# Expert weights in tiles of 2 MiB, with 16 KiB in a row, in a decoder block on one core

## The chip, the core and the metric

The kernel runs on one core of a Trainium2 chip. The metric is the device time of one execution in microseconds; the time of the kernel before is the median of three runs. A profile of one execution gives the trace from which the rows below are read.

## The reference

One block of a decoder for 256 tokens of 1024 features, in float32. What matters here is its last third, a mixture of experts:

```python
def hier_moe(xn, w_rg, b_rg, w_re, b_re, w_e_gate, w_e_up, w_e_down):
    ...                                   # group: top 1 of 8; expert: top 2 of 8 in it
    def expert_block(a):
        xb, e = a
        hdn = jax.nn.silu(xb @ w_e_gate[e]) * (xb @ w_e_up[e])
        return hdn @ w_e_down[e]
    ...

h = h + token_mixer(rmsnorm(h), ...)           # gated unit over tokens beside causal attention
h = h + mem_cross_attention(rmsnorm(h), ...)
h = h + hier_moe(rmsnorm(h), ...)              # 64 experts: gate and up 1024 x 512, down 512 x 1024
return rmsnorm(h, norm_final)
```

The weights of the first two thirds are 48 MiB, those of the 64 experts 384 MiB, 6 MiB each.

## The kernel before, in words

**Dense stage.** The products of the mixers and of the cross-attention read their weights in 48 pieces of 1 MiB (8 KiB in each of 128 partitions), in the order of the list ORDER (line 68). Each piece is split on ScalarE and VectorE into a rounded part and its rest (`split`, line 233), and three passes on PE make the product (`feature_out`, line 282, `token_out`, line 300).

**Expert stage.** 16 groups of four experts (GE = 4, line 39). Each expert has 32 slots for tokens, so four experts fill the array's columns side by side, 32 each. For a group PE gathers its tokens (line 815), makes gate and up (`pg` and `pu`, line 965: eight chunks of rows, for each chunk four experts), turns the hidden rows (line 852), makes the down product (`py`, line 986) and adds the weighted rows to the tokens' sums (line 862). In most groups the innermost loop of both products goes over the four experts. In the last group the down product goes by three blocks of columns (BLOCKS, line 48), and there the loop goes over the experts, and for each over two chunks of rows (line 1031). Its sums then run through the final norm (lines 905 to 935). Products that nothing reads (`keep_warm`, line 175) stand before and between the last ones (lines 1028, 1035, 1038).

**Loads.** All weights form one list, `pieces` (lines 98 to 115): for a group four experts' gate and up, each half the rows of an expert (four rows of 2 KiB that follow each other in HBM, 8 KiB), then the down weights (two rows of 4 KiB in two places). The last group's down pieces are cut by blocks of columns, with rows of 2 and 1 KiB. `pump` (line 119) issues the next pieces on SyncE's queue (SP) as long as slots are free; `take` and `done` count them. Weights and activations share one ring of slots, NBIG = 20 of 8 KiB in a partition (line 80), and from the expert stage on there are NBIG2 = 3 more (line 722). Caps (`cap`, CAPS) hold the number of slots with weights down in the dense stage. SP works in order: a transfer that waits for its slot, or for an earlier transfer to land, holds back all that is queued behind it. At the start, `xT` and the first two pieces come in parts by chunks of rows (FIRST, line 51), then piece 2, then the residual `h` (line 164), then more pieces. `h` is needed for the first rms (`squares`, line 268, called from line 354).

Of the kernel before, what the change touches and what calls it, by code (L numbers as in the profile page):

```python
# [29 lines left out]
P = 128  # L30
# [23 lines left out]

# The dense weights in pieces of 1 MiB: as they are packed, and in the order of their use.
PACKED = [("v", 4), ("u", 4), ("wa", 4), ("g", 8), ("k", 4), ("q", 4), ("va", 4), ("wb", 4), ("wo", 4),
          ("xk", 2), ("xq", 2), ("xv", 2), ("xo", 2)]


def _dense_index(name, i):  # L60
    base = 0
    for n, c in PACKED:
        if n == name:
            return base + i
        base += c
# [9 lines left out]
def block_kernel(ctx, tc, x, xt, mem, memt, wp, par, wrp, brt, wsp, bsp, rel, oneh, gfin, weg, weu, wed, out):  # L75
# [12 lines left out]
    def slot(name, shape=(P, 2048), dtype=F32, kind="a"):  # L88
# [9 lines left out]
    pieces = [(wp[_dense_index(name, i)], (P, 2048)) for name, i in ORDER]  # L98
    def up_pieces(w, g, h):
        """Half h of the rows of four experts: a piece per expert, or per chunk of rows at the start."""  # L100
        ws = w[g * GE:(g + 1) * GE].rearrange("e (p k) n -> p e k n", p=P)[:, :, 4 * h:4 * h + 4, :]
        if g == 0 and h == 0 and w is weg:
            return [(ws[:, :, k], (P, GE, EH)) for k in range(4)]
        return [(ws[:, e], (P, 4, EH)) for e in range(GE)]

    def down_pieces(g):
        """Halves of the rows; at the end also by blocks of columns."""
        ws = wed[g * GE:(g + 1) * GE].rearrange("e (j p) n -> p e j n", p=P)
        return [(ws[:, e, 2 * h:2 * h + 2, lo:hi], (P, 2, hi - lo))
                for lo, hi in (BLOCKS if g + 1 == NGRP else [(0, D)]) for h in range(2) for e in range(GE)]  # L110

    for g in range(NGRP):
        for h in range(2):
            pieces += up_pieces(weg, g, h) + up_pieces(weu, g, h)
        pieces += down_pieces(g)
    loaded = {}
    nxt, used, cap = [0], [0], [6]

    def pump():
        while nxt[0] < len(pieces):  # L120
# [6 lines left out]
            src, shape = pieces[nxt[0]]  # L127
            t = slot("w", shape, kind=kind)
            nc.sync.dma_start(t, src)  # L129
            loaded[nxt[0]] = (t, kind)  # L130
            nxt[0] += 1

    taken = []

    def take():
        i = used[0]
        used[0] += 1
        t, kind = loaded.pop(i)
        taken.append(kind)
        return t  # L140
# [12 lines left out]
    xT = slot("xT", (P, KC, T))  # L153
    for k0, k1 in FIRST:
        i = k0 // 4
        if k0 % 4 == 0:
            loaded[i] = (slot("w", kind="w"), "w")
        cs = slice(k0 % 4 * 512, (k0 % 4 + k1 - k0) * 512)
        nc.sync.dma_start(xT[:, k0:k1], xt[:, k0:k1])
        nc.sync.dma_start(loaded[i][0][:, cs], pieces[i][0][:, cs])  # L160
    nxt[0] = 2
    cap[0] = 3
    pump()
    nc.sync.dma_start(h, x.rearrange("(t p) d -> p t d", p=P))
    cap[0] = 6
# [9 lines left out]
    def keep_warm(ps, n):  # L175
        """Products that nothing reads: the array's clock falls to half when it idles."""
# [37 lines left out]
    with ExitStack() as ph:  # L214
# [11 lines left out]
        def after_split():  # L226
            """What the block traces on the two engines queues behind the newest split."""
# [5 lines left out]
        def split(src, shape):  # L233
            """A weight block as a float32r part and the float32r rest."""
# [8 lines left out]
        def parts(hi, lo, src, scale=None):  # L243
            """src (PSUM or SBUF) * scale, split into float32r parts."""
# [8 lines left out]
        def to_features(xs, gam, hi, lo, pairs):  # L253
            """Token-major [P, 2, D] -> feature-major parts [P, KC, T], times gam, for pairs of chunks."""
# [13 lines left out]
        def squares(src, ss):  # L268
            """Sum of squares of src [P, 1024] to ss [P, 1]."""
# [3 lines left out]
        def row_of(r, name):  # L273
            """r [P tokens, 2] as a row of 256 on every partition."""
# [7 lines left out]
        def feature_out(c, xh, xl, evac, between=()):  # L282
            """x @ W, feature-major: two 128-feature tiles of a piece of W."""
# [16 lines left out]
        def token_out(c, kpieces, xh, xl, evac, before=None, step=SPLIT_K // 2):  # L300
            """x @ W, token-major: 512 columns, K over pieces of 4 chunks."""
# [24 lines left out]
        xh, xl = slot("xh", (P, KC, T), F32R), slot("xl", (P, KC, T), F32R)  # L326
# [9 lines left out]
        wb = slot("wb", (P, 2, D))  # L336
        wspt = wb[:, 0].rearrange("p (g t) -> p g t", g=8)
        bspt = wb[:, 1].rearrange("p (g t) -> p g t", g=8)
        nc.sync.dma_start(wb[:, 0], wsp)
        nc.sync.dma_start(wb[:, 1], bass.AP(tensor=bsp.tensor, offset=bsp.offset, ap=[[0, P], [1, D]]))  # L340
# [4 lines left out]
        vg = slot("vg", (P, 2, D))  # L345
# [15 lines left out]
        drop()  # L361
# [15 lines left out]
        uT = slot("uT", (P, KC, T))  # L377

# [20 lines left out]
        bias = slot("bias", (P, HEADS, 256))  # L399
# [5 lines left out]
        gates = [slot("g0", (P, KC, T)), slot("g1", (P, KC, T))]  # L405
# [8 lines left out]
        uh, ul = slot("uh", (P, KC, T), F32R), slot("ul", (P, KC, T), F32R)  # L414
# [31 lines left out]
        drop(3)  # L446

# [1 line left out]
        va = slot("va", (P, 2, D))  # L449
# [6 lines left out]
        kT = slot("kT", (P, HEADS, T))  # L456
        qT = slot("qT", (P, HEADS, T))
# [8 lines left out]
        ah, al = slot("ah", (P, HEADS, T), F32R), slot("al", (P, HEADS, T), F32R)  # L466
# [44 lines left out]
        for i in range(12):  # L511
# [12 lines left out]
            if i == 7:  # L524
                drop(2)
                cap[0] = CAPS[0]
            if 3 <= i <= 10:
                mix_values(i - 3)
        drop(6)

# [1 line left out]
        cap[0] = CAPS[1]  # L532
        pump()
        mm_, mT = slot("mem", (P, 2, D)), slot("mT", (P, KC, T))
        nc.sync.dma_start(mT, memt)
        nc.sync.dma_start(mm_, mem.rearrange("(t p) d -> p t d", p=P))
        mh, ml = slot("mh", (P, KC, T), F32R), slot("ml", (P, KC, T), F32R)
# [10 lines left out]
        drop(4)  # L548
# [4 lines left out]
        cap[0] = CAPS[2]  # L553
        for c in range(2):
            token_out(c, 2, mh, ml, add_h)
        nh, nl = slot("nh", (P, KC, T), F32R), slot("nl", (P, KC, T), F32R)
# [7 lines left out]
        drop(4)  # L564
        cap[0] = CAPS[3]
        pump()

# [1 line left out]
        kv = slot("kv", (P, 2, D))  # L569
        kxT = kv[:, 0].rearrange("p (h t) -> p h t", h=XHEADS)  # L570
        vx = kv[:, 1].rearrange("p (m n) -> p m n", m=2)
# [4 lines left out]
        yh, yl = slot("yh", (P, KC, T), F32R), slot("yl", (P, KC, T), F32R)  # L576
        cap[0] = CAPS[4]
# [14 lines left out]
        pr4 = slot("pr", (P, XHEADS, 2, T))  # L592
# [55 lines left out]
        drop(2)  # L648
        cap[0] = NBIG
        pump()  # L650
        token_out(0, 2, nh, nl, vx_evac, beside_vx)
        drop(2)
# [51 lines left out]
        drop(2)  # L704
# [28 lines left out]
    # constants of the routing  # L733
# [10 lines left out]
    G.iota(io64, pattern=[[-1, NE]], base=NE, channel_multiplier=0, allow_small_or_imprecise_dtypes=True)  # L744
# [450 lines left out]
```

## Time and profile before

| | |
|---|---|
| time, median of 3 runs | 1257.06 us (1256.94 to 1258.0) |
| span of the profiled execution | 1254.8 us |
| PE busy | 954.4 us, 76% |
| PE weight loads busy | 525.8 us, 42% |
| VectorE, ScalarE busy | 258.1 us, 224.9 us |
| GpSimd busy | 21.5 us, 52 instructions |
| DMA packets, bytes | 90014, 463.31 MB |
| read from HBM over the span | 370 GB/s |

The table's busy times are means over the whole span, and the kernel has two stages of different kind, so the slices, the windows and the chain of work say more. In the slices each digit is the busy share of a fortieth of the span in tenths. Times of PE's instructions have modelled ends and overlap. [...]

### The profile page before, as it was taken

Reading aid. Unit: us, or ns where it says so; the run is one execution under the profiler, and the core shown is the slowest. Engines: PE = TensorE matmul, PEld = TensorE weight load, DVE = VectorE, ACT = ScalarE, POOL = GpSimd, SP = SyncE. Lnnn points to the kernel's source line nnn. Section 1 sums busy time; section 2 is a strip of 40 time slices with the busy share of each in tenths; the row PEclk is TensorE's granted clock in tenths of the full one; section 3 lists DMA queues with packets and bytes.
Section 4 is the critical chain, followed back from the end, with each engine's and each line's share of the span. In section 5 each row is a group of like instructions: output and inputs, shape, how many; then the busy total and the mean of one; then the engine's idle time right before and its main releaser. Section 6 shows DMA issues by size and latency. Waiting matters only on the chain.

```text
span 1254.8 us, 14523 instructions
## 1 busy us (share of the span) xinstructions
PE 954.4 (76%) x6167; PEld 525.8 (42%) x6167; DVE 258.1 (21%) x480; ACT 224.9 (18%) x372; POOL 21.5 (2%) x52
## 2 busy tenths in 40 slices
PE   8999999999897667667575758484848576756676
PEld 7998999898443122121222222222222222221223
DVE  5656676776200000000000000000000000000002
ACT  6455554664100000000000000000000000000002
POOL 0010000000000000000000000000000000000000
PEclk9999999999998888787888878888979787878889
DMA  9696258848999999999999999999999999999995
GB/s 352 252 359 232 102 198 316 291 142 294 389 416 418 416 418 415 420 413 420 413 421 413 421 413 422 413 421 413 421 413 420 414 420 415 418 416 417 417 404 179
DMA packets 90014, 463.31 MB, mean 369 GB/s; under 512 B 7857, under 2 KB 14809, under 8 KB 51674
## 3 DMA queue, kind: packets, MB, share of 16 engines
q1 hardware_dynamic: 89658, 461.96, 91.6%
q8 instruction: 49, 0.80, 0.3%
q10 hardware_dynamic: 288, 0.39, 0.1%
q14 instruction: 19, 0.16, 0.0%
HBM read 461.26 MB, written 2.63 MB: 370 GB/s over the span
## 4 chain that ended last, share of the span: by engine, by line
DMA 59%; PE 37%; SPq 2%; DVE 1%; ACT 1%; issue 0%; DVEq 0%; ACTq 0%
DMA w<-in_weg 30%; DMA w<-in_weu 16%; DMA w<-in_wed 12%; PE acc L294 5%; PE acc L296 5%; PE acc L295 5%; PE pg L965 3%; PE py L986 3%; PE pu L965 3%; PE acc L315 2%; PE acc L316 2%; PE acc L314 2%; SPq L129 2%; PE xp L815 1%; PE a L862 1%; PE a L1009 1%
## 5 line engine op out<-in xcount | busy, mean ns | idle before, releaser
L965 PE MATMUL pg<-w,xg 128*32 128x512 f32 x1024 | 213.7, 701 | 212.5 <-DMA w<-in_weg 212.4
L965 PE MATMUL pu<-w,xg 128*32 128x512 f32 x1024 | 186.0, 647 | 51.0 <-DMA w<-in_weu 50.8
L965 PEld LDWEIGHTS pg<-w,xg 128*32 128x32 f32 x1024 | 42.3, 124 | 343.8 <-DMA w<-in_weg 258.7
L849 DVE SCALAR_TENSOR_TENSOR ws<-pu,cw,ws 128x512 f32<-128x512 f32 x16 | 12.0, 751 | 744.0 <-ACT ws L848 414.3
L986 PE MATMUL py<-w,ws 128*32 128x512 f32 (+1 forms) x1056 | 161.9, 693 | 0.3 <-ACT ws L853 0.3
L239 DVE TENSOR_TENSOR lo<-w,hi 128x1024 fp32r<-128x1024 f32 (+1 forms) x102 | 120.6, 1183 | 68.6 <-ACT hi L237 68.2
L237 ACT ACTIVATE hi<-w 128x1024 fp32r<-128x1024 f32 (+1 forms) x102 | 102.7, 1008 | 115.3 <-PE acc L295 78.7
L965 PEld LDWEIGHTS pu<-w,xg 128*32 128x32 f32 x1024 | 45.0, 117 | 165.5 <-DMA w<-in_weu 91.3
L294 PE MATMUL acc<-xh,hi 128*128 128x256 f32 x320 | 91.7, 287 | 0.0
L848 ACT ACTIVATE ws<-pg,cw 128x512 f32<-128x512 f32 x16 | 11.0, 687 | 445.3 <-PE pu L965 277.9
L295 PE MATMUL acc<-xl,hi 128*128 128x256 f32 x320 | 90.5, 283 | 0.0
L296 PE MATMUL acc<-xh,lo 128*128 128x256 f32 x320 | 90.4, 283 | 0.0
L986 PEld LDWEIGHTS py<-w,ws 128*32 128x32 f32 x1056 | 45.7, 122 | 101.2 <-issue 94.9
L860 ACT ACTIVATE ws<-py 128x512 f32<-128x512 f32 (+1 forms) x33 | 19.3, 584 | 306.1 <-PE py L986 306.1
L815 PE MATMUL xp<-gt,h 128*128 128x128 f32 x512 | 62.3, 280 | 0.6 <-DVE gt L799 0.6
L815 PEld LDWEIGHTS xp<-gt,h 128*128 128x128 f32 x512 | 60.3, 196 | 3.3 <-issue 2.5
L294 PEld LDWEIGHTS acc<-xh,hi 128*128 128x128 f32 x320 | 61.2, 191 | 0.7 <-issue 0.6
L295 PEld LDWEIGHTS acc<-xl,hi 128*128 128x128 f32 x320 | 61.3, 192 | 0.1
L296 PEld LDWEIGHTS acc<-xh,lo 128*128 128x128 f32 x320 | 61.2, 191 | 0.0
L862 PE MATMUL a<-ws,cw 128*128 128x512 f32 (+1 forms) x128 | 58.6, 599 | 1.2 <-ACT ws L860 1.2
L862 PEld LDWEIGHTS a<-ws,cw 128*128 128x128 f32 x128 | 22.9, 189 | 37.2 <-issue 22.0
L816 DVE TENSOR_TENSOR xg<-xp,prm 128x512 f32<-128x512 f32 (+2 forms) x35 | 22.6, 646 | 61.0 <-PE xp L815 61.0
(288 smaller groups left out, 905.0 us busy)
## 6 DMA issues: line engine op xcount, KB each, us to landing
w<-in_weg SPq DMA_DIRECT2D x128, 1024.0 KB, 19.8
w<-in_weu SPq DMA_DIRECT2D x128, 1024.0 KB, 19.9
w<-in_wed SPq DMA_DIRECT2D x120, 1024.0 KB, 20.0
w<-in_wp SPq DMA_DIRECT2D x46, 1024.0 KB, 9.9
w<-in_wed SPq DMA_DIRECT2D x8, 512.0 KB, 15.4
w<-in_wed SPq DMA_DIRECT2D x16, 256.0 KB, 6.3
w<-in_wp SPq DMA_DIRECT2D x3, 512.0 KB, 8.1
skew<-brow SPq DMA_DIRECT2D x1, 1536.0 KB
```

The costliest lines, as they stand in the source:

```text
L129: nc.sync.dma_start(t, src)
L237: newest[0] = S.activation(hi, src, AF.Copy)
L239: newest[1] = V.tensor_sub(lo, src, hi.bitcast(F32))
L294: PE.matmul(ps[:, m], wh[:, k - k0], xh[:, k], start=(k == 0), stop=False)
L295: PE.matmul(ps[:, m], wh[:, k - k0], xl[:, k], start=False, stop=False)
L296: PE.matmul(ps[:, m], wl[:, k - k0], xh[:, k], start=False, stop=(k == KC - 1))
L314: PE.matmul(ps[t], xh[:, k, ts], wh[:, j], start=first, stop=False)
L315: PE.matmul(ps[t], xh[:, k, ts], wl[:, j], start=False, stop=False)
L815: PE.matmul(xp[:, k], h[:, t, (k0 + k) * P:(k0 + k + 1) * P], gt[:, t], start=(t == 0), stop=(t == 1))
L862: mm = PE.matmul(dst[t], cw[:, t * P:(t + 1) * P], ws[:, lo:hi], start=first, stop=last)
L965: PE.matmul(po_[es_], xg[:, 4 * hh + k, es_], wk[:, e] if by_chunk else wg[e][:, k], start=(hh == 0 and k == 0), stop=(hh == 1 and k == 3))
L986: return PE.matmul(py[es_], hT[:, j, es_], wd, start=(j == 0), stop=(j == 3))
```

## The change

The host packs the weights anew, and the kernel loads them in tiles of 2 MiB, with 16 KiB in a row for each partition.

- *Experts.* A tile holds, for four experts at once, a quarter of the rows of gate, of up or of down: 12 tiles in a group, in HBM one behind the other (`wq`). The last group's down weights are packed by the blocks of columns (`wz`): two tiles for block 0, one for block 1, and one for block 2, which is loaded in four transfers of 512 KiB with 4 KiB in a row.
- *Dense.* Two of the 1 MiB pieces form a tile, in the order of their use. The first comes in chunks as before, the second in two halves, and `h` is issued behind them.
- *Buffers.* The ring has 11 slots of 16 KiB, and one more in the expert stage. Activations of 8 KiB are put in one slot by pairs. `ws`, the rows beside the hidden product, gets a buffer of its own. CAPS count tiles. The memory that is set aside for GpSimd's own DMA descriptors goes from its default to 128 bytes in a partition.
- *Order on PE.* Gate is done before up for all rows, tile by tile; the down products of the last group go over chunks, and for each chunk over the experts. The fillers between the last products fall away; six before the last block stay.
- *Branch for tokens beyond 32 of an expert* (taken only where there are such tokens): it finds its expert's rows by a row number, for which one more iota is made.

The diff, cut to its core:

```diff
-NBIG = 20
-NBIG2 = 3
+NBIG = 11
+NBIG2 = 1
+SCRATCH = 128
-CAPS = (9, 12, 14, 15, 14)
+CAPS = (5, 6, 7, 7, 8)
-WARM_END = (6, 3)
+WARM_END = 6
...
+    def pair(name, dtype=F32, shape=(KC, T)):
+        t = slot(name, (P, 2) + shape, dtype)
+        return t[:, 0], t[:, 1]
...
+    tiles = [((P, 2, 2048), [(slice(0, 2), wp[i])], 2) for i in range(len(ORDER) // 2)]
+    tiles += [((P, GE, 1024), [(slice(0, GE), wq[g, i])], 1) for g in range(NGRP) for i in range(12 if g + 1 < NGRP else 8)]
+    tiles += [((P, 2, 2048), [(slice(0, 2), wz[i].rearrange("p (j n) -> p j n", j=2))], 1) for i in range(2)]
+    tiles += [((P, 4, 1024), [(slice(0, 4), wz[2].rearrange("p (j n) -> p j n", j=4))], 1)]
+    tiles += [((P, 4, 1024), [(j, wz[3][:, j * 1024:(j + 1) * 1024]) for j in range(4)], 1)]
...
-    nxt[0] = 2
-    cap[0] = 3
+    nxt[0] = 1
+    cap[0] = 2
+    tiles[1][1][:] = [(i, wp[1][:, i]) for i in range(2)]
     pump()
     nc.sync.dma_start(h, x.rearrange("(t p) d -> p t d", p=P))
-    cap[0] = 6
+    cap[0] = CAPS[0]
     pump()
...
-    xh, xl = slot("xh", (P, KC, T), F32R), slot("xl", (P, KC, T), F32R)
+    xh, xl = pair("xhl", F32R)
...
+    ws = mt("ws", [P, 1536])
...
-        for hh in range(2):
-            for po_ in (pg, pu):
-                by_chunk = g == 0 and hh == 0 and po_ is pg
-                wg = [] if by_chunk else [take() for _ in range(GE)]
...
+        for po_ in (pg, pu):
+            for c in range(4):
+                w = take().rearrange("p e (k n) -> p e k n", k=2)
+                for k in range(2):
                     for e in range(GE):
                         es_ = slice(SLOTS * e, SLOTS * (e + 1))
+                        PE.matmul(po_[es_], xg[:, 2 * c + k, es_], w[:, e, k], start=(c + k == 0), stop=(c == 3 and k == 1))
+                done()
+                if g == 0 and po_ is pg and c < 3:
+                    gather_chunks(xg, gt, 2 * c + 2, 2)
...
-            for hh in range(2):
-                wd = [take() for _ in range(GE)]
-                for j in range(2):
+            for j in range(4):
+                wd = take()
...
                     if at_end:
-                        idle = ps_t.tile([P, P], F32, tag="t", name="idle")
-                        keep_warm(idle, WARM_END[0])
-                    for hh in range(2):
-                        wd = [take() for _ in range(GE)]
-                        for e, j in [(e, j) for e in range(GE) for j in range(2)]:
-                            mm = down(2 * hh + j, py, e, wd[e][:, j])
-                            if at_end and j and e < hh * 3:
-                                with tc.issue_after(mm.ins):
-                                    keep_warm(idle, 1)
-                        if at_end and not hh:
-                            with tc.issue_after(mm.ins):
-                                keep_warm(idle, WARM_END[1])
+                        keep_warm(ps_t.tile([P, P], F32, tag="t", name="idle"), WARM_END)
+                    js = 4096 // (GE * (hi - lo))
+                    for j0 in range(0, 4, js):
+                        wd = take().rearrange("p j (e n) -> p j e n", e=GE)
+                        for j in range(js):
+                            for e in range(GE):
+                                mm = down(j0 + j, py, e, wd[:, j, e])
                         done()
...
+    up = lambda w: w.reshape(NGRP, GE, P, 4, 2 * EH).transpose(0, 3, 2, 1, 4)
+    wdn = w_e_down[0].reshape(NGRP, GE, 4, P, D).transpose(0, 2, 3, 1, 4)
+    wq = np.concatenate([up(w_e_gate[0]), up(w_e_up[0]), wdn], axis=1)
```

## Rows read from the trace of the kernel before

**Rows 1.** The page's slices of PE and DMA, 40 of 31.4 us.

```profile
PE   8999999999897667667575758484848576756676
DMA  9696258848999999999999999999999999999995
```

**Rows 2.** The page's chain that ended last, by engine and by line.

```profile
DMA 59%; PE 37%; SPq 2%; DVE 1%; ACT 1%; issue 0%; DVEq 0%; ACTq 0%
DMA w<-in_weg 30%; DMA w<-in_weu 16%; DMA w<-in_wed 12%; PE acc L294 5%; PE acc L296 5%; PE acc L295 5%; PE pg L965 3%; PE py L986 3%; PE pu L965 3%; PE acc L315 2%; PE acc L316 2%; PE acc L314 2%; SPq L129 2%; PE xp L815 1%; PE a L862 1%; PE a L1009 1%
```

**Rows 3.** Windows: length, busy us (instructions), granted clock, DMA share, GB/s.

```profile
320.00:324.00 4.00, 4.00 (x33) 2.07 (x32) 1.65 (x8) 0.00 (x0) 0.76 (x2) 1.00 0.84 276
...
880.00:940.00 60.00, 37.10 (x246) 13.40 (x242) 2.56 (x5) 2.87 (x5) 0.76 (x2) 0.87 1.02 417
1206.00:1214.00 8.00, 6.62 (x30) 1.49 (x30) 0.00 (x0) 0.00 (x0) 0.00 (x0) 0.57 1.01 412
...
1238.00:1248.00 10.00, 8.22 (x46) 4.12 (x42) 1.12 (x7) 2.02 (x8) 0.00 (x0) 1.00 0.03 8
```

**Rows 4.** The DMA view from 938 to 966 us, up weights alone.

```profile
DMA packets 1617, 11.80 MB, mean 421 GB/s; under 512 B 178, under 2 KB 178, under 8 KB 178
```

**Rows 5.** The DMA view from 972 to 988 us, down weights alone.

```profile
DMA packets 1663, 6.53 MB, mean 408 GB/s; under 512 B 100, under 2 KB 100, under 8 KB 1633
```

**Rows 6.** SP's timeline: start, length; down transfers of two groups.

```profile
896.86 21.85 SPq L129 DMA_DIRECT2D w<-in_wed  x8
...
957.29 21.65 SPq L129 DMA_DIRECT2D w<-in_wed  x8
```

**Rows 7.** SP's own waits: us in total, times, longest.

```profile
SPq L129 <- DMA w<-in_weg: 239.2, 114, 3.4
```

**Rows 8.** The page's DMA issues: KB each, median us to landing.

```profile
w<-in_weg SPq DMA_DIRECT2D x128, 1024.0 KB, 19.8
```

**Rows 9.** SP's timeline where the expert stage begins.

```profile
299.77 22.26 SPq L129 DMA_DIRECT2D w<-in_wed  x8
323.75 7.88 SPq L129 DMA_DIRECT2D w<-in_weg  x4
```

**Rows 10.** The timeline at the start, around the first rms.

```profile
7.59 0.71 SPq L164 DMA_DIRECT2D h<-in_x  x1
...
19.14 1.04 ACT L271 ACTIVATE junk<-h 128x1024 bf16<-128x1024 f32 x1
...
22.99 2.36 DVE L239 TENSOR_TENSOR lo<-w,hi 128x1024 fp32r<-128x1024 f32 x2
...
25.14 0.48 PE L314 MATMUL acc<-hi,xh 128*128 128x512 f32 x1
```

**Rows 11.** The view of the tile `h`, 0 to 60 us.

```profile
DMA to landing us min/median/max: 11.3/11.3/11.3
```

**Rows 12.** The chain that ended last, in order of time, its end.

```profile
1197.05 20.16 DMA w<-in_weu
...
1223.48 6.32 PE py L986 x31
...
1230.48 1.98 PE a L862 x4
...
1236.27 1.34 PE idle L178 x12
...
1239.05 0.86 PE idle L178 x6
...
1240.89 0.42 PE idle L178 x2
...
1244.11 0.99 PE py L986 x4
```

**Rows 13.** The same chain in the first group.

```profile
349.58 6.87 PE py L986 x64
```

**Rows 14.** The page's DMA queues: packets, MB, share of 16 engines.

```profile
q8 instruction: 49, 0.80, 0.3%
```

More of the change, by code (lines that the diff above doesn't have):

```diff
@@ L74, in block_kernel @@
 @with_exitstack
-def block_kernel(ctx, tc, x, xt, mem, memt, wp, par, wrp, brt, wsp, bsp, rel, oneh, gfin, weg, weu, wed, out):
+def block_kernel(ctx, tc, x, xt, mem, memt, wp, par, wrp, brt, wsp, bsp, rel, oneh, gfin, wq, wz, out):
     nc = tc.nc
@@ L93, in slot @@
         return pool.tile(list(shape), dtype, tag="big", name=f"{name}_{made[0]}")
+    def pair(name, dtype=F32, shape=(KC, T)):
+        t = slot(name, (P, 2) + shape, dtype)
+        return t[:, 0], t[:, 1]
     def drop(n=1, kind="a"):
         live[kind] -= n
[L98 to L115, printed above, removed]
+    tiles = [((P, 2, 2048), [(slice(0, 2), wp[i])], 2) for i in range(len(ORDER) // 2)]
[3 more added lines that the diff above has]
+    tiles += [((P, 4, 1024), [(j, wz[3][:, j * 1024:(j + 1) * 1024]) for j in range(4)], 1)]
     loaded = {}
-    nxt, used, cap = [0], [0], [6]
+    nxt, used, cap = [0], [0], [3]
     def pump():
-        while nxt[0] < len(pieces):
+        while nxt[0] < len(tiles):
             if extra and live["x"] < NBIG2:
@@ L126, in pump @@
                 break
-            src, shape = pieces[nxt[0]]
+            shape, transfers, pieces = tiles[nxt[0]]
             t = slot("w", shape, kind=kind)
-            nc.sync.dma_start(t, src)
-            loaded[nxt[0]] = (t, kind)
+            for at, src in transfers:
+                nc.sync.dma_start(t[:, at], src)
+            loaded[nxt[0]] = (t, kind, pieces)
             nxt[0] += 1
     taken = []
+    halves = [0]
     def take():
[L136 to L140, printed above, removed]
+        t, kind, pieces = loaded[used[0]]
+        at = halves[0]
+        halves[0] = (at + 1) % pieces
+        if not halves[0]:
+            del loaded[used[0]]
+            used[0] += 1
+            taken.append(kind)
+        return t[:, at] if pieces > 1 else t
     def done():
@@ L744, in block_kernel @@
     G.iota(io64, pattern=[[-1, NE]], base=NE, channel_multiplier=0, allow_small_or_imprecise_dtypes=True)
+    row64 = mt("row64", [P, NE])
+    G.iota(row64, pattern=[[12 * P * GE, NGRP], [1, GE]], base=0, channel_multiplier=0, allow_small_or_imprecise_dtypes=True)
+    rows = wq.rearrange("g c p e n -> (g c p e) n")
     tri = mt("tri", [P, 2, P], BF16)
@@ L1074, in block_kernel, with expert_tile @@
             V.tensor_sub(jobs, jobs, o64)
-            eif, eii = mt("eif", [P, 1]), mt("eii", [P, 1], I32)
-            V.tensor_scalar(eif, b64, -1.0, float(NE), op0=ALU.mult, op1=ALU.add)
-            V.tensor_copy(eii, eif)
-            ei = nc.values_load(eii[0:1, 0:1], engines=(mybir.EngineType.SP,), min_val=0, max_val=NE - 1)
+            row, rowi = mt("eif", [P, 1]), mt("eii", [P, 1], I32)
+            V.tensor_mul(t64, o64, row64)
+            V.tensor_reduce(row, t64, axis=AX.X, op=ALU.add)
+            V.tensor_copy(rowi, row)
+            row0 = nc.values_load(rowi[0:1, 0:1], engines=(mybir.EngineType.SP,), min_val=0,
+                                  max_val=(NGRP - 1) * 12 * P * GE + GE - 1)
+            def expert_tile(c0):
+                w = big.tile([P, 4, 1024], F32, tag="big", name="wo")
+                for c in range(4):
+                    nc.sync.dma_start(w[:, c], rows[bass.ds(row0 + (c0 + c) * P * GE, P, step=GE)])
+                return w
             gt, gw = mt("gt", [P, 2, P]), mt("gw", [P, 2, P])
@@ L1102, in block_kernel @@
             py = [ps_t.tile([P, 512], F32, tag="t", name="pyo") for _ in range(2)]
-            for hh in range(2):
-                wo = big.tile([P, 2, D], F32, tag="big", name="wdo")
-                nc.sync.dma_start(
-                    wo, wed[bass.ds(ei, 1)].rearrange("o (j p) n -> p (o j) n", p=P)[:, 2 * hh:2 * hh + 2, :])
-                for j in range(2):
-                    for n in range(2):
-                        PE.matmul(py[n], hT[:, 2 * hh + j], wo[:, j, n * 512:(n + 1) * 512],
-                                  start=(hh == 0 and j == 0), stop=(hh == 1 and j == 1))
+            wo = expert_tile(8)
+            for j in range(4):
+                for n in range(2):
+                    PE.matmul(py[n], hT[:, j], wo[:, j, n * 512:(n + 1) * 512], start=(j == 0), stop=(j == 3))
             for n in range(2):
```

155 lines of the change are left out of this document (66 added, 89 removed).

## The prediction

> **What bounds the kernel now.** I read the page first: the slices, then the chain of work that ended last. PE is full in the first quarter of the span and then falls to six or seven tenths, while DMA goes from uneven to nine tenths and stays there to the end [rows 1]. The chain says the same by time: 59% of it is transfers, nearly all of them expert weights, and the PE part is mostly the dense products of lines 294 to 316 [rows 2]. So there are two stages: a dense one (to about 320 us) in which PE sets the pace and weights are loaded ahead, and an expert one in which PE waits for weights. The windows agree: from 880 to 940 us PE is busy 37.10 of 60 us, and the 16 DMA engines are busy all the time [rows 3].
>
> What is the expert stage's pace made of? A group of four experts is 24 MiB: 16 MiB up (gate and up), in rows of 8 KiB, and 8 MiB down, in rows of 4 KiB. The DMA view of a stretch with up weights alone shows 421 GB/s, that of one with down weights alone 408 GB/s [rows 4, 5]. 16.78 MB at 421 and 8.39 MB at 408 are 39.9 + 20.6 = 60.4 us, and the first down transfers of two neighbouring groups are issued 957.29 - 896.86 = 60.4 us apart [rows 6]. The two rates therefore explain the whole stage, and no wait on a buffer is needed for it. SP's waits in pump (line 129) are mostly for an earlier transfer to land [rows 7]; with 19.8 us from issue to landing and 2.5 us per MiB, eight transfers are in flight [rows 8].
>
> **Part 1: longer runs.** Per engine (a sixteenth of the rate) 8192 bytes take 311.3 ns and 4096 bytes 160.6 ns. Two packets of 4 KiB cost 9.9 ns more than one of 8 KiB: a fixed price per packet of about 10 ns on 150.7 ns per 4 KiB. If a run of 16 KiB goes out as one packet, it takes 2 x 311.3 - 9.9 = 612.7 ns, which is 428 GB/s over 16 engines. A group then takes 25.17 MB / 428 GB/s = 58.8 us instead of 60.4: 1.6 us, of which 1.0 comes from the down weights. From the end of the first group's load to the last up weight there are 14 whole groups and one group's 16 MiB of up weights (0.6 us): 14 x 1.59 + 0.6 = **22.9 us saved**. No row shows a weight packet of 16 KiB, so both ends: with no price per packet the slope alone gives 435 GB/s (57.9 us a group, 13.9 us better still), and with nothing gained beyond 8 KiB 421 GB/s (59.8 us, 14.1 us worse). I take the straight line, since both rows lie on it and one step further is a short way.
>
> The trace shows a price of about 10 ns per packet [rows 4, 5]. [...]
>
> **Part 2: half as many transfers, twice as large.** Eight in flight are then 16 MiB of 24 MiB of buffers; four tiles remain for PE, which needs one per 4.9 us. Cost nothing, covered by the queue: the next transfer is always there. [...] Issue time halves and is off the path.
>
> **Part 3: the start of the expert stage.** Both kernels fill their buffers while PE finishes the dense part, then wait for PE's first release. Before, the first group's 24 MiB are issued by 322 us and the second group starts at 323.75 [rows 9], with DMA at 0.84 in between [rows 3]. After, there are 12 tiles of 2 MiB, also 24 MiB; the first tile comes free only after two chunks of rows, about 1 us later, and each then frees in 3 us against 4.9 us of transfer. I take 0, with 1 MiB either way as bound: 2.5 us. What hides the coarser buffers in the dense stage is depth: beside six pairs of activations five tiles are left, 10 MiB; the dense stage spends 48 MiB in some 310 us, 6.5 us per MiB, so 65 us of PE's work lie ahead. Without that cover each late tile would cost up to its 4.9 us.
>
> **Part 4: the first microseconds.** `h` is now issued behind 4 MiB of weights instead of 3. It landed at 7.59 + 11.3 = 18.9 us, and the squares began at 19.14, so nothing is to spare there [rows 10, 11]. 1 MiB later is 2.5 us. The squares stand ahead of the next splits on ACT and the rms chain ahead of them on DVE: the split that ended its first half at about 24.2 us would end at 26.7, while PE takes it from 25.14, its second part one product later. PE stalls about **1.2 us**, bounds 0 and 2.5. PE bounds this stage, so all that follows shifts.
>
> **Part 5: the tail.** The last up weights land at 1217.2, DMA ends near 1238 [rows 3, 12], and the last down product ends at 1245.1: 27.9 us, most of it PE's. Block 0 takes 6.32 us for 31 records shown, while in other groups 64 take 6.87 [rows 12, 13]: there the expert changes with each product, and four run side by side; in the last group two products of one expert follow each other. Fillers between the last products take 0.86 + 3 x 0.42 = 2.1 us. After: the expert changes each time again, those fillers are gone (the first, 1.34 us, stay), and runs of 2 and 1 KiB become 16 and 4 KiB. Tiles land 4.9, 9.8 and 14.7 us after the last up weights, and the four pieces of the last by 14.7 + 4 x 1.29 = 19.8. PE: block 0's second tile 9.8 + 1.7, copy and combination 0.6 + 2.0 = 14.1; block 1 from 14.7, 1.7 + 0.4 + 1.1 = 17.9; fillers 19.3; block 2 by 21.0. That is at a granted clock of 1.00; PE now waits between tiles, and where it did so before, from 1206 to 1214 us, the granted clock was 0.57 [rows 3], so up to 25. I take 22.5: **5.4 us saved**, bounds 2 and 7. The 9.7 us behind the last product stay.
>
> **Parts at nothing.** `ws` as one buffer: it is written again only after the next group's up products, which stand behind this group's combination on PE. The iota for the branch: one of POOL's 52 operations, mean 0.41 us, read by no one here. The pairs and the order of packing on the host: no instruction.
>
> **The sum.** 22.9 + 5.4 - 1.2 = 27.1 us off the profiled execution's 1254.8 us: 1227.7. The median of the runs is 2.3 us above that span, for what lies around it: **1230.0 us**.
>
> **The rivals.**
> - *Runs beyond 8 KiB earn nothing.* The gap between 421 and 408 could come from the down weights' addresses (rows 4 KiB apart, in two places) and not from packets; or a run is cut into packets of 8 KiB. For it: one gap alone is seen, between two tensors. Against it: the difference is the same with both engines and stretches saturated. Then 421 everywhere: 1244 us. [...]
> - *No price per packet is left*, 435 GB/s: 1216 us.
> - *Slower: a run of 16 KiB leaves as four packets of 4 KiB, or is as slow as they are.* Then the up weights fall from 421 to 408 GB/s: 61.7 us a group, 2.9 more than forecast, 14.7 times: 42 us more, 1272 us. It turns slower than before from 60.7 us a group, 415 GB/s (632 ns per 16 KiB). For it: the only packets of 16 KiB are the 49 instruction loads on a queue of their own, 0.3% of 16 engines' span, which is above 1 us each [rows 14]; they go elsewhere and were mixed with weight packets. Against it: runs of 8 KiB go out whole, 1617 packets for 11.8 MB with 178 small ones [rows 4].
> [...]
> - *The change loses in the dense stage what it gains*: a stall of some 25 us by coarse buffers, 1255 us.
>
> **How the numbers follow.** Forecast (1222 to 1238) 0.62; 8 KiB rate 0.17; no price 0.08; cut packets 0.06; half clock 0.04; dense stall 0.03. A difference below 0.2% can't be told from none. Faster: 0.62 + 0.17 + 0.08 = 0.87; same 0.03; slower 0.10. The range takes in both rates with the bounds of the tail and the start: 1216 - 1.6 - 1.2 = 1213, and 1244 + 3.4 = 1248; the last three cases lie outside.
>
> **What would show it.** Some 40,000 packets in place of 90,014, most of them of 16 KiB, and the mean rate of the expert stage near 428, flat from group to group. A group's period of 58.8 us. `h` landing near 21.4 and a gap of a microsecond on PE at 25. The last product about 22 us behind the last up weights. Wrong would be: a rate of 421 or less, windows in the middle in which DMA is below nine tenths (PE or buffers bind), or PE gaps before 310 us.

## The result and the profile after

The changed kernel takes **1235.6 us** (median of four runs, 1235.38 to 1240.17) against 1257.26 for the kernel before, run beside it: a ratio of 0.984, 95% interval 0.9823 to 0.9856. The forecast was 1230.0, so it came out faster, as forecast, within the range of 1213 to 1248, and 5.6 us above the forecast. The profiled execution has a span of 1233.7 us, 21.1 us less than before; the sum had said 27.1.

The page of the changed kernel: the slices of PE, DMA and GB/s (40 of 30.8 us), the packets of the whole span, and the chain that ended last, by engine.

```profile
PE   8998999999989675757576675666665656675765
...
DMA  9875338755999999999999999999999999999995
GB/s 352 369 278 216 137 113 308 280 198 205 368 428 428 427 428 427 428 428 426 429 426 429 428 426 429 427 429 427 427 428 427 428 427 428 429 426 428 427 426 226
DMA packets 37355, 463.27 MB, mean 376 GB/s; under 512 B 4226, under 2 KB 7082, under 8 KB 9643
...
DMA 68%; PE 29%; DVE 1%; ACT 1%; issue 0%; SPq 0%; DVEq 0%; ACTq 0%
```

From the twelfth slice to the last but one the rate is flat at 426 to 429 GB/s, where before it was 421 for up weights and 408 for down weights [rows 4, 5]. There are 37,355 packets in place of 90,014, and the share of transfers in the chain has grown from 59% to 68% [rows 2].

A window in the middle (length, busy us of PE, PE's loads, VectorE, ScalarE, GpSimd, granted clock, DMA share, GB/s), SP's wait for transfers (us in total, times, longest), and the page's DMA issues (KB each, median us to landing):

```profile
880.00:940.00 60.00, 36.61 (x242) 11.82 (x242) 2.56 (x5) 2.87 (x5) 0.76 (x2) 0.89 1.01 427
...
SPq L113 <- DMA w<-in_wq: 740.7, 164, 6.0
...
w<-in_wq SPq DMA_DIRECT2D x188, 2048.0 KB, 39.1
```

PE has as much slack as before [rows 3], DMA has none, and eight transfers of 2 MiB are in flight (39.1 us at 4.9 us each, where it was 19.8 at 2.5 [rows 8]). The expert stage is thus as the prediction drew it. From the first gather of the expert stage (`xp`) to the product on the last up weights (`pu`, 1201.36 in the changed kernel, shown with the tail below) it took 873.96 us against 897.81 before: **23.9 us saved**, 22.9 forecast. The chains of the changed kernel (first line) and of the kernel before:

```profile
327.40 1.16 PE xp L805 x8
...
319.44 1.16 PE xp L815 x8
...
1217.25 3.62 PE pu L965 x26
```

The longer runs alone explain somewhat less. From 400 to 1150 us the kernel before moves 312.88 MB and the changed one 320.71 MB; at these rates a group's 25.17 MB takes 60.33 and 58.86 us, 1.47 us less, which over the 14.67 groups of Part 1 is, as an estimate, 21.6 us. The other 2 us lie at the start of the stage, where Part 3 had put nothing.

**What was lost.** The first gather starts 8.0 us later than before, 327.40 against 319.44. The timelines of the two kernels show where. First, the changed kernel at the start (start, length, engine, line; in brackets the idle time before, and what ended it; `hi` is a weight block's rounded part):

```profile
9.46 0.39 SPq L154 DMA_DIRECT2D h<-in_x  x1
11.56 0.50 PE L304 MATMUL acc<-hi,xhl 128*128 128x512 f32 x1 [1.12 <-ACT hi L227]
22.16 1.06 ACT L261 ACTIVATE junk<-h 128x1024 bf16<-128x1024 f32 x1 [1.88 <-DMA h<-in_x]
```

`h` is issued 1.9 us later than before and lands after 12.7 us, at 22.2; the squares start 3.0 us later than in [rows 10]. Behind them PE runs 1.96 us later than in the kernel before. Only half of that comes with `h`: PE was already 1.0 us late at 11.56, where it waited for the split of one of the first pieces of the weights, and 0.9 us come on at 26 to 27 us, behind the squares. The other 6 us arise in one place, the gates (`gt` is the evacuation on VectorE, `gates` the sigmoid on ScalarE that reads it). The changed kernel's timeline:

```profile
62.58 0.69 DVE L398 TENSOR_TENSOR gt<-acc,rxB 128x512 f32<-128x512 f32 x1 [0.62 <-PE acc L286]
68.34 0.69 DVE L398 TENSOR_TENSOR gt<-acc,rxB 128x512 f32<-128x512 f32 x1 [0.69 <-PE acc L286]
...
91.04 1.06 ACT L227 ACTIVATE hi<-w 128x1024 fp32r<-128x1024 f32 x1 [2.71 <-PE acc L285]
...
93.92 1.06 ACT L227 ACTIVATE hi<-w 128x1024 fp32r<-128x1024 f32 x1 [1.82 <-PE acc L285]
94.99 1.28 ACT L401 ACT_TABLE_LOAD   x1
96.29 2.57 ACT L401 ACTIVATE gates<-gt,prm 128x256 f32<-128x256 f32 x6
97.23 0.69 DVE L398 TENSOR_TENSOR gt<-acc,rxB 128x512 f32<-128x512 f32 x1 [0.99 <-ACT gates L401]
97.97 0.38 PE L284 MATMUL acc<-xhl,hi 128*128 128x256 f32 x1 [3.97 <-DVE gt L398]
```

and the same place in the kernel before:

```profile
66.38 0.69 DVE L409 TENSOR_TENSOR gt<-acc,rxB 128x512 f32<-128x512 f32 x1 [0.69 <-PE acc L296]
...
83.51 1.28 ACT L412 ACT_TABLE_LOAD   x1
...
85.74 0.69 DVE L409 TENSOR_TENSOR gt<-acc,rxB 128x512 f32<-128x512 f32 x1 [0.99 <-ACT g L412]
```

An evacuation takes a finished product out of PE's accumulator. Two evacuations go through, the third waits: the buffers that it needs are freed by sigmoids, and the sigmoids stand behind the weight splits in ScalarE's queue, although ScalarE is idle there for 1.8 and 2.7 us at a time, waiting for PE to free a split buffer. Counted from the first evacuation, ScalarE does eight splits before the first sigmoid in the kernel before, and eleven in the changed one. Meanwhile PE fills its four accumulators, and with eleven splits it runs out of them: 3.97 us of idle time, which the kernel before doesn't have. Windows of the changed kernel show what follows (columns as above):

```profile
94.00:98.00 4.00, 0.03 (x1) 0.03 (x1) 1.92 (x2) 3.97 (x7) 0.00 (x0) 1.00 0.00 0
98.00:102.00 4.00, 3.84 (x18) 3.57 (x19) 3.83 (x6) 2.81 (x6) 1.28 (x1) 0.57 0.00 0
102.00:106.00 4.00, 4.00 (x36) 4.00 (x35) 3.24 (x7) 2.34 (x6) 2.60 (x2) 1.00 0.29 53
```

After the break the granted clock is 0.57 on average for 4 us, and 18 products run where 36 do at 1.00. So 4.0 us of stall bring some 2 us more: the lag behind the kernel before, taken at the same instructions, grows from 2.0 to 8.0 us there and stays at 8.0 to the end of the dense stage.

**The tail**, PE's timeline of the changed kernel from the last up weights on:

```profile
1201.36 3.35 PE L954 MATMUL pu<-w,xg 128*32 128x512 f32 x16 [1.25 <-DMA w<-in_wq]
...
1207.01 1.92 PE L970 MATMUL py<-w,ws 128*32 128x512 f32 x16 [0.25 <-ACT ws L843]
1211.17 3.57 PE L970 MATMUL py<-w,ws 128*32 128x512 f32 x16 [2.24 <-DMA w<-in_wz]
1215.46 1.98 PE L852 MATMUL a<-ws,cw 128*128 128x512 f32 x4 [0.73 <-ACT ws L850]
1217.38 1.93 PE L970 MATMUL py<-w,ws 128*32 128x256 f32 x32
1219.81 1.13 PE L852 MATMUL a<-ws,cw 128*128 128x256 f32 x4 [0.51 <-ACT ws L850]
1220.78 1.50 PE L168 MATMUL idle<-ident 128*128 128x128 f32 x12
1222.21 1.93 PE L970 MATMUL py<-w,ws 128*32 128x256 f32 x32
```

From 1201.36 to the end of the last product, 1224.15, it is 22.8 us; before 27.9, forecast 22.5. Behind the last product lie 9.5 us (9.7 before). The account of the span closes: expert stage, later start, tail and what lies behind it, 23.85 - 7.96 + 5.05 + 0.16 = 21.1 us.

### The profile page after: what moved, and what is told of

Its sections match the earlier page's. It is cut to its first block, busy times and chain, and to the rows that moved or that the text cites. A ratio compares the mean times of both kernels' runs of the same rounds, so it can differ in the third digit from the quotient of the medians.

```text
span 1233.7 us, 14100 instructions
## 1 busy us (share of the span) xinstructions
PE 927.9 (75%) x6155; PEld 503.3 (41%) x6155; DVE 258.0 (21%) x480; ACT 224.8 (18%) x372; POOL 21.7 (2%) x53
## 2 busy tenths in 40 slices
DMA packets 37355, 463.27 MB, mean 376 GB/s; under 512 B 4226, under 2 KB 7082, under 8 KB 9643
## 4 chain that ended last, share of the span: by engine, by line
DMA 68%; PE 29%; DVE 1%; ACT 1%; issue 0%; SPq 0%; DVEq 0%; ACTq 0%
DMA w<-in_wq 63%; PE acc L285 5%; PE acc L284 5%; PE acc L286 5%; DMA w<-in_wz 3%; PE acc L305 2%; PE acc L306 2%; PE acc L304 2%; PE pg L954 1%; PE xp L805 1%; PE py L970 1%; DMA h<-in_x 1%; PE pu L954 1%; PE a L991 1%; PE a L852 1%; DMA xw<-in_xt 1%
## 5 line engine op out<-in xcount | busy, mean ns | idle before, releaser
L954 PE MATMUL pu<-w,xg 128*32 128x512 f32 x1024 | 172.6, 804 | 118.2 <-DMA w<-in_wq 118.2
L954 PE MATMUL pg<-w,xg 128*32 128x512 f32 x1024 | 146.2, 696 | 81.6 <-DMA w<-in_wq 81.6
L970 PE MATMUL py<-w,ws 128*32 128x512 f32 (+1 forms) x1056 | 138.6, 661 | 68.6 <-DMA w<-in_wq 59.3
L954 PEld LDWEIGHTS pu<-w,xg 128*32 128x32 f32 x1024 | 34.5, 129 | 253.1 <-DMA w<-in_wq 193.1
L954 PEld LDWEIGHTS pg<-w,xg 128*32 128x32 f32 x1024 | 30.4, 119 | 186.5 <-DMA w<-in_wq 125.4
L970 PEld LDWEIGHTS py<-w,ws 128*32 128x32 f32 x1056 | 32.9, 116 | 154.4 <-DMA w<-in_wq 90.8
L284 PE MATMUL acc<-xhl,hi 128*128 128x256 f32 x320 | 92.0, 288 | 4.0 <-DVE gt L398 4.0
L285 PE MATMUL acc<-xhl,hi 128*128 128x256 f32 x320 | 90.9, 284 | 0.0
L286 PE MATMUL acc<-xhl,lo 128*128 128x256 f32 x320 | 90.8, 284 | 0.0
L284 PEld LDWEIGHTS acc<-xhl,hi 128*128 128x128 f32 x320 | 61.5, 192 | 4.9 <-DVE gt L398 4.2
L285 PEld LDWEIGHTS acc<-xhl,hi 128*128 128x128 f32 x320 | 61.6, 192 | 0.1
L286 PEld LDWEIGHTS acc<-xhl,lo 128*128 128x128 f32 x320 | 61.5, 192 | 0.0
## 6 DMA issues: line engine op xcount, KB each, us to landing
w<-in_wq SPq DMA_DIRECT2D x188, 2048.0 KB, 39.1
w<-in_wz SPq DMA_DIRECT2D x3, 2048.0 KB, 39.1
h<-in_x SPq DMA_DIRECT2D x1, 1024.0 KB, 12.7
```

Source lines behind the costliest of these rows:

```text
L284: PE.matmul(ps[:, m], wh[:, k - k0], xh[:, k], start=(k == 0), stop=False)
L285: PE.matmul(ps[:, m], wh[:, k - k0], xl[:, k], start=False, stop=False)
L286: PE.matmul(ps[:, m], wl[:, k - k0], xh[:, k], start=False, stop=(k == KC - 1))
L954: PE.matmul(po_[es_], xg[:, 2 * c + k, es_], w[:, e, k], start=(c + k == 0), stop=(c == 3 and k == 1))
L970: return PE.matmul(py[es_], hT[:, j, es_], wd, start=(j == 0), stop=(j == 3))
```

## The experiments

The kernel before, run beside each of these kernels, took 1256.7 to 1257.3 us, so the medians can be set side by side.

**Length of a run.** The expert tiles are packed differently, everything else stays. With runs of 4 KiB:

```
-    ... [(slice(0, GE), wq[g, i])] ...
+    ... [(slice(0, GE), wq[g, i].rearrange("e p n -> p e n"))] ...      # wq packed [g, tile, expert, row, n]
```

> The changed kernel with one thing undone: the tiles are still 2 MiB and each is still one transfer of a contiguous 2 MiB of memory, but within it the four experts' rows lie apart, so that a run is 4 KiB instead of 16 KiB. Theory (a fixed price of about 10 ns per packet, Part 1): 4 KiB packets at 408 GB/s in every group, some 122,000 packets, a group in 61.7 us instead of 58.8, 14.7 times 2.9 = 42 us more: 1278 us. Rival (the gap between 408 and 421 GB/s came from where the down weights lay, or from the size of a transfer): still 428 GB/s and 1236 us.

With runs of 8 KiB, `wq` packed [g, tile, pair of experts, row, two experts]:

> As the run with 4 KiB, but with the experts in pairs: 2 MiB transfers with runs of 8 KiB. Theory (price per packet): 421 GB/s in every group, 59.8 us a group, 14.7 times 1.0 = 14 us more than the changed kernel: 1250 us, a third of what 4 KiB costs. Rival (size of a transfer or place in memory decides): 428 GB/s and 1236 us.

Measured: **1274.89 us** (1274.22 to 1276.89; ratio 1.0145, 1.0129 to 1.016) and **1247.07 us** (1246.54 to 1251.07; 0.992, 0.9904 to 0.9935). The DMA view from 880 to 940 us of the run with 4 KiB, of that with 8 KiB, and of the changed kernel:

```profile
DMA packets 6169, 24.53 MB, mean 409 GB/s; under 512 B 189, under 2 KB 189, under 8 KB 6165
```

```profile
DMA packets 3278, 25.27 MB, mean 421 GB/s; under 512 B 195, under 2 KB 195, under 8 KB 195
```

```profile
DMA packets 1766, 25.63 MB, mean 427 GB/s; under 512 B 201, under 2 KB 201, under 8 KB 201
```

Same bytes, same transfers of 2 MiB, same buffers: the rate follows the run, and both rates are those that the kernel before showed for its 4 and 8 KiB runs in transfers of 1 MiB [rows 4, 5]. The place of the down weights is thus excluded as a cause. One thing moved along: a transfer lands after 24.0 and 32.8 us in these two runs instead of 39.1, so fewer than eight are in flight. It isn't what sets the rate, since the DMA share of this window is 1.03 and 1.01, as full as the changed kernel's 1.01; why fewer are in flight was not looked into. In an engine's time for 16 KiB: four packets 641 ns (16 x 16384 B / 409 GB/s), two 623, one 614. Each packet less is worth, as an estimate from these three, 9 ns, close to the 10 that Part 1 had read from two rows. The run with 4 KiB was to cost 42 us and cost 39.3, that with 8 KiB 14 and cost 11.5.

**Size of a transfer.** Each expert tile in two transfers of 1 MiB, in two ways, by halves of the partitions and by even and odd ones:

```
-                nc.sync.dma_start(t[:, at], src)
+                ...                                               # for the expert tiles only, one of the two:
+                for ps in (slice(0, 64), slice(64, P)):           # size1m
+                for ps in (slice(0, P, 2), slice(1, P, 2)):       # even1m
+                    nc.sync.dma_start(t[ps, at], src[ps])
```

> The changed kernel with its runs of 16 KiB, but each expert tile fetched by two transfers of 64 partitions, 1 MiB each as in the kernel before. Theory (only the length of a run counts, Part 2 at nothing): 428 GB/s, 1236 us within 2, landing time down from 39 to about 20 us because eight transfers are then 8 MiB. Rival (the larger transfer is what is faster): 413 to 421 GB/s as before, 1250 to 1256 us.

Measured: 1850.33 us, far outside what either theory had expected. Its four executions differ widely (1697.84, 1755.3, 1945.36 and 2002.19 us); the trace is of the longest. So the second form was run:

> As the run with two transfers of 64 partitions for each expert tile, which fell to 218 GB/s, but here one transfer takes the even partitions and the other the odd ones, so that 1 MiB still reaches over the whole width of the buffers; runs stay 16 KiB. Theory (the size of a transfer costs nothing; the half rate came from writing to one half of the partitions at a time): 427 GB/s, 1236 us within 3. Rival (transfers of 64 partitions, or of 1 MiB with runs of 16 KiB, are slow as such): 218 GB/s and some 1700 to 2000 us again.

Measured: **1237.09 us** (1235.83 to 1241.89; ratio 0.9838, 0.9823 to 0.9853). The DMA view from 880 to 940 us, halves first, then even and odd, each with its landing time:

```profile
DMA packets 998, 13.08 MB, mean 218 GB/s; under 512 B 199, under 2 KB 199, under 8 KB 199
...
w<-in_wq SPq DMA_DIRECT2D x12, 1024.0 KB, 38.3
```

```profile
DMA packets 1951, 25.61 MB, mean 427 GB/s; under 512 B 387, under 2 KB 387, under 8 KB 387
...
w<-in_wq SPq DMA_DIRECT2D x24, 1024.0 KB, 19.6
```

The second settles the question: 1 MiB or 2 MiB per transfer, 8 or 16 MiB in flight, the rate is 427 GB/s. Part 2 was right to put the size at nothing. The first shows something else, told below.

**The stall at the gates.** The sigmoids of a piece are queued ahead of the splits of the third piece behind it:

```
+            with tc.issue_after(opened[c - 3].ins) if c >= 3 else ExitStack():   # opened[c]: last sigmoid of piece c
                 feature_out(c, xh, xl, gate_evac, ...)
```

> The changed kernel with one thing added: on ScalarE the sigmoids of gate piece c-3 are queued ahead of the weight splits of piece c, so that they no longer stand behind eleven splits. Nothing else moves. Theory (the new 4 us gap of PE at 98 us and the clock's fall behind it come from ScalarE's order: the evacuations on VectorE wait for buffers that the sigmoids free, the four accumulators fill, PE stops): the gap goes, the first gather moves from 327.4 to about 321.3 us, and the time falls by 6 us to 1229.5. Rival (the gap comes from late weights or from the table load of the sigmoid): no change, 1235.6 us, the gap only moves.

Measured: **1228.91 us** (1227.92 to 1232.26; ratio 0.9782, 0.9769 to 0.9796), 6.7 us below the changed kernel, and the intervals of the two ratios don't touch. VectorE's timeline and a window of this run:

```profile
67.88 0.69 DVE L399 TENSOR_TENSOR gt<-acc,rxB 128x512 f32<-128x512 f32 x1 [0.68 <-PE acc L286]
74.59 0.69 DVE L399 TENSOR_TENSOR gt<-acc,rxB 128x512 f32<-128x512 f32 x1 [4.93 <-issue]
82.94 0.68 DVE L399 TENSOR_TENSOR gt<-acc,rxB 128x512 f32<-128x512 f32 x1
...
80.00:100.00 20.00, 20.00 (x169) 20.00 (x168) 13.72 (x18) 11.61 (x16) 4.43 (x3) 1.00 0.69 252
```

The evacuations now come piece by piece, PE is busy for all of 80 to 100 us at a clock of 1.00, and the first gather starts at 321.06 in place of 327.40, 6.3 us earlier. The theory holds with its number, and late weights or the table load are excluded.

Why did the order change at all, when no line of it was touched? A likely reason, a guess of the author's: the build places each engine's instructions by its own estimate of when their inputs are there, and the change loads the gates' weights earlier. From the start it holds up to five tiles, 10 MiB, where the kernel before held six pieces, 6 MiB. A run that goes back to three tiles, 6 MiB, with nothing put in order by hand:

```
-CAPS = (5, 6, 7, 7, 8)
+CAPS = (3, 6, 7, 7, 8)
```

> The changed kernel with one number changed: until the keys and queries three weight tiles are held ahead instead of five. This loads the weights of the gates later, and in the order that the build then writes for ScalarE the first sigmoid stands behind eight splits, as in the kernel before, instead of eleven; no edge is added by hand. Theory (ScalarE's order makes the gap, and it was the earlier weights that changed the order): the gap of 4 us at 98 us goes, the gather starts near 321.5 us, 1229.5 us. Rival (the shallower prefetch is short of tiles): gaps of PE on weights in the first 120 us, no gain or slower, 1236 to 1245 us.

Measured: 1233.65 us (1232.24 to 1234.8; ratio 0.9811, 0.9796 to 0.9826), 2 us gained where 6 were expected, and its interval just touches that of the changed kernel. The first gather starts at 324.97, not at 321.5. Timelines of ScalarE and PE:

```profile
85.98 1.28 ACT L401 ACT_TABLE_LOAD   x1
87.28 2.58 ACT L401 ACTIVATE gates<-gt,prm 128x256 f32<-128x256 f32 x6
...
97.26 0.39 PE L284 MATMUL acc<-xhl,hi 128*128 128x256 f32 x1 [1.84 <-ACT hi L227]
98.52 0.39 PE L286 MATMUL acc<-xhl,lo 128*128 128x256 f32 x1 [0.76 <-DVE lo L229]
```

The first sigmoid stands behind eight splits again, and the wait for an accumulator is gone. But now twelve sigmoids and two other operations stand ahead of the next split, and PE waits 2.6 us for splits instead, which the kernel before doesn't. It doesn't wait for a transfer there, so the rival (short of tiles) falls. The depth of prefetch does steer the order of ScalarE's queue, and each order has its own price; the time that was expected did not come. That the build's estimate moved the sigmoids by three splits is not shown.

**`h` behind 3 MiB instead of 4**, on top of the run gates:

```
-    tiles[1][1][:] = [(i, wp[1][:, i]) for i in range(2)]
+    tiles[1][1][:] = [(0, wp[1][:, 0])]
     pump()
     nc.sync.dma_start(h, x.rearrange("(t p) d -> p t d", p=P))
+    nc.sync.dma_start(loaded[1][0][:, 1], wp[1][:, 1])
```

> The changed kernel with the sigmoids queued early as in the run gates (1228.9 us) and, in addition, h issued behind 3 MiB of weights and x instead of 4, as in the kernel before. Theory (Part 4: 1 MiB ahead of h delays the squares on ScalarE and PE by one to two microseconds): h lands 2.5 us earlier, the first gather moves from 321.06 to between 319.1 and 320.1 us, and the time falls by 1 to 2 us to 1227 to 1228. Rival (the second half of the second tile is then late by as much, PE waits for it instead): no change, 1228.9.

Measured: 1228.83 us (1226.94 to 1229.42; ratio 0.977, 0.9756 to 0.9783). The squares start at 20.04 us and the gather at 320.23. Runs with `h` behind 4 MiB and no stall had the gather at 321.06, 321.69 and 321.94 (gates, and fillmove and nofill below), so the stage is 0.8 to 1.7 us shorter, a little less than the 1 to 2 expected; but the median is the same within 0.1 us, which is the rival's time. Single executions differ by more than the effect, and whether the microsecond reaches the end stays open.

**The tail by itself**, in the kernel before; layout and transfers stay as they were:

```
-                        for e, j in [(e, j) for e in range(GE) for j in range(2)]:
+                        for j, e in [(j, e) for j in range(2) for e in range(GE)]:
                             mm = down(2 * hh + j, py, e, wd[e][:, j])
-                            ... (the fillers between the last products)
```

> The kernel before with one thing changed, the order of the last group's down products: the expert changes with each product instead of every second one, and the fillers between the products of the last block are gone; layout, transfers and buffers are those of before. Theory (the tail's gain is the order and the fillers, not the longer runs): DMA still ends near 1238 us, the last product then ends about 1.5 us later at 1239.5 instead of 1245.1, and the time falls by 5.5 us to 1251.5. Rival (the tail waits for the short runs of the last transfers, so order is worth nothing): within 1 us of 1256.8.

Measured: **1252.2 us** (1251.84 to 1252.8) against 1256.78: ratio 0.9961, 0.9947 to 0.9974, 4.6 us. PE's timeline:

```profile
1218.33 5.32 PE L965 MATMUL pu<-w,xg 128*32 128x512 f32 x26 [1.49 <-DMA w<-in_weu]
...
1226.26 4.56 PE L986 MATMUL py<-w,ws 128*32 128x512 f32 x32 [0.25 <-ACT ws L853]
...
1238.58 2.86 PE L986 MATMUL py<-w,ws 128*32 128x256 f32 x32
```

From the last up weights to the last product it is now 1241.4 - 1218.3 = 23.1 us, against 27.9 before and 22.8 in the changed kernel. Order and fillers together thus give 4.8 of the 5.1 us; the longer runs of the last transfers give next to nothing. How the 4.8 divide between the order and the fillers was not run.

**Further down the tail**, both on top of the run gates. The six fillers ahead of the last block go:

> The run gates (1228.9 us) without the six fillers that stand ahead of the last block's products. In it all transfers have landed before the fillers begin, so PE's chain sets the end. Theory: 1.4 us less, 1227.5 us, granted clock still 1.00 over the last products, since PE works without a longer break from the first down product on. Rival (the fillers cover the wait for the combination's copy or hold the clock): no change, or slower by up to 2 us.

Measured: **1227.39 us** (1226.92 to 1228.12; ratio 0.9764, 0.9751 to 0.9778), 1.5 us below the run gates, with the clock at 1.00 over the last products. It is the lowest median here, though its interval overlaps that of gates, and in the traces the last product ends 21.5 us after the last up weights in gates and 21.1 us in nofill. So the 1.4 us are likely, but not shown apart from the spread. Then ten fillers where PE waits for the second tile:

> The run nofill (1227.39 us) with ten fillers put where PE waits for the second tile of the last group's first block, 2.9 us in which the clock fell, so that its sixteen products took 3.28 us instead of the 1.92 us of the first tile's sixteen. Theory: the clock stays whole, those products take 1.92 us, and the end comes 1.3 us earlier: 1226.1 us. Rival (the fillers run into the landing of the tile, or the granted clock falls all the same): no change, 1227.4 us.

Measured: 1227.73 us (1226.91 to 1229.44; ratio 0.9768, 0.9755 to 0.9782): no gain. PE's timeline:

```profile
1204.01 2.50 PE L168 MATMUL idle<-ident 128*128 128x128 f32 x20
1206.44 1.92 PE L972 MATMUL py<-w,ws 128*32 128x512 f32 x16
```

The products do take 1.92 us now. But counted from the last up weights (1196.00) the tile was due at 1205.8, 9.8 us on, so the fillers held them up by 0.6; the last product ends 20.4 us after the last up weights against 21.1 in nofill. The 0.7 us that remain can't be told from no change.

**Beyond 16 KiB.** Only the weights' way into the buffers, with runs of 16 KiB and of 32 KiB:

> Only the weights' way into the buffers: 96 transfers of 2 MiB with runs of 16 KiB into ten buffers, 201 MB, no products; the output is filled with zeros, so the whole computation is left out. A control for the next run. Theory: 428 GB/s as in the changed kernel, since PE has no part in the rate. Rival (PE's reads of the buffers or the waits of pump held it back): above 430 GB/s.

> The same 201 MB, again without any of the computation, as 48 transfers of 4 MiB with runs of 32 KiB into five buffers. Theory (a fixed price of about 10 ns per packet goes on holding): a packet of 32 KiB takes 2 times 612.7 less 9.9 = 1215.5 ns, 431 GB/s, some 6,100 packets of weights. Rival (a run is cut into packets of 16 KiB): 428 GB/s and 12,300 packets. Another rival (the price is gone beyond 16 KiB): 435 GB/s.

Measured, one execution each: spans of 475.9 and 473.1 us. The DMA view from 100 to 400 us, 16 KiB first:

```profile
DMA packets 8890, 129.42 MB, mean 431 GB/s; under 512 B 990, under 2 KB 990, under 8 KB 990
```

```profile
DMA packets 4459, 129.94 MB, mean 433 GB/s; under 512 B 493, under 2 KB 493, under 8 KB 493
```

Runs of 32 KiB leave whole, and the span is 2.8 us shorter on 201 MB. Each engine sends 384 packets less for it, so 7 ns each; the rates of the two windows, 431 and 433 GB/s, give about 5 ns. Both are below the 9 ns of the shorter runs. With one execution each, and half as many buffers for the longer runs, that a price is left is likely and its size is open. The control gave its rival's figure: 16 KiB runs reach 431 GB/s without the products and 428 in the kernel, so the theory that PE and pump have no part in the rate is not borne out; what takes the 0.7% there was not tried.

## Why the prediction was right, and where it was off

- **What bounds the kernel, Part 1: right.** The price per packet, read from the gap between two tensors, held at 4, 8 and 16 KiB: 428 GB/s forecast, 426 to 429 measured; 22.9 us forecast, about 21.6 by the rates. The rivals that gave 421 (1244), 435 (1216) and cut packets (1272) are excluded by the packet count and the rate. PE as the bound, which the chances hold at 0.04 as half clock, is excluded by its 36.61 busy us of 60 at a mean clock of 0.89; no run shows the whole stage at half clock.
- **Part 2: right to put it at nothing**, by the run with even and odd partitions.
- **Part 3, start of the expert stage:** 0 forecast. From the gather to the last up weights the gain is 23.9 us, some 2 us above what the rates give, within the bound of 2.5. What brings them was not looked into; that the whole lies within 1.0 us of Part 1's 22.9 is in part two misses that cancel.
- **Part 3, the coarse buffers in the dense stage: the step that failed.** It asked only whether a tile comes too late, and named depth as the cover. No tile came too late. But earlier tiles changed the order of ScalarE's queue, and PE stopped for want of an accumulator. "The pairs and the order of packing on the host: no instruction" was true and beside the point: no instruction was added, one was moved in a queue. The forecast had no term for this; it measured 6.0 us in the trace, and 6.7 us came back when it was undone. The rival "stall in the dense stage" was there, with its 25 us sized for a stall on weights, and the text had named PE gaps before 310 us as a sign of being wrong: that sign came up. That the time still fell within the range is owed to the range's width, which was set for the DMA rates, not for this loss.
- **Part 4, `h`:** right in size; 1.2 us forecast, 0.9 in the trace of the changed kernel, though not as one gap of a microsecond on PE at 25 us. Another 1.0 us that the forecast had no term for stands ahead of `h`, at 11.56 us. `h` landed at 22.2 instead of the 21.4 expected, since its issue slipped too.
- **Part 5, the tail: right in size**, 5.1 us against 5.4, and the run on the kernel before confirms that the order on PE and the fillers make it. One detail was wrong: at the end PE's own chain decides, not the landing of the last four pieces, so that the fillers that stayed are on the path; without them the median was 1.5 us lower, with overlapping intervals.
- **The clock in the tail:** it had been weighed in with 1.5 us over the 21.0 at a clock of 1.00; the trace shows that it cost time at one place, where the second tile's products took 3.57 us instead of 1.92 after a wait of 2.24 (granted clock 0.54 from 1211.2 to 1214.8 us, 1.00 from 1207 to 1209). The last up products took 3.35 us (clock 0.54 from 1201.0 to 1204.6 us), but PE then waited for the second tile all the same.

In sum, against the forecast: 1.0 us more from the expert stage (runs and start together) and 0.2 behind the last product, 0.4 less from the tail and 6.8 more lost in the dense stage, which is the 6.0 us by which the span missed.

## What to carry to other kernels

Where a stage waits for transfers all the time, read the rate at each run length and fit a price per packet; what other run lengths gained or cost then followed here to within a fifth. Between 1 and 2 MiB, with eight in flight, the size of a transfer was free (427 GB/s at both) as long as it didn't sit in one half of the partitions (218 GB/s). A change of buffers or prefetch also moved instructions in queues that it never mentions (eleven splits ahead of the first sigmoid in place of eight): compare each engine's order before and after, and look for an operation that frees a buffer and stands behind work that isn't due. Count every break of PE with what the lower clock takes after it (here some 2 us after 3.97 us, 1.65 us after 2.24).

## What the runs showed that was not expected

**Half the partitions, half the rate.** Transfers into partitions 0 to 63 and 64 to 127 in turn run at 218 GB/s with all 16 engines busy (DMA share 1.01), transfers into the even and the odd partitions at 427; size, run length, number of partitions and number in flight are the same. So which partitions a transfer covers decides here. In most of the execution with the two halves, with eight in flight (38.3 us from issue to landing at 4.8 us per MiB), the rate stayed low (215 to 232 GB/s in its slices from 350 to 1450 us), but from 1450 to 1700 us the slices show 272 to 315 GB/s, and the other three executions were up to 304 us shorter. So the half rate doesn't hold all the time; what lifts it was not looked into.

**A break of PE cost about half as much again:** 3.97 us of idle time and then a clock of 0.57 over 4 us made 6.0 us. In the tail a wait of 2.24 us cost 1.65 us more, by which the products behind it (3.57 us) were longer than the 1.92 us of the same work at a clock of 1.00; the granted clock over them was 0.54.
